# Sparse attention scores two heads at a time, low-key products in row halves, values eight units behind

## The chip, the cores and the metric

The kernel runs on one core of a Trainium2 chip. The core has five engines that work from instruction queues of their own: TensorE (PE in the profile; its weight loads are listed as PEld), VectorE (DVE), ScalarE (ACT), GpSimd (POOL) and SyncE (SP), which here issues nearly all DMA transfers. Each engine takes its instructions in a fixed order and waits at the first one whose inputs or buffers are not ready. The metric is the time of one execution on the device, in microseconds (us); lower is better.

## The reference

Two identical layers work on 512 tokens of width 1024. Each mixes three branches, adds them under sigmoid gates, and goes on to a gated feed-forward network of width 2816. The branches are two chunked gated linear attentions (HGRN2 with 4 heads of 128, GLA with 4 heads of 64) and a sparse attention of 8 heads of 64 in 2 key groups. The sparse attention is what the change is about. Cut to its core:

```python
for a block of 128 queries, t its token numbers:                     # 4 blocks
    p_c = masked_softmax(q @ kc, cmp_end <= t);  o_c = p_c @ vc      # 31 compressed keys
    # 16 blocks of 64 keys may be chosen, and 512 tokens have only 8: all of the past is chosen
    p_s = masked_softmax(q @ k_sel, tok <= t);   o_s = p_s @ v_sel   # "selected" branch
    p_w = masked_softmax(q @ k_win, causal);     o_w = p_w @ v_win   # "window" branch (512 wide)
out = gates[0]*o_c + gates[1]*o_s + gates[2]*o_w                     # per token and head
m = g[0]*(y_hg @ w_br_hg) + g[1]*(y_gla @ w_br_gla) + g[2]*(y_nsa @ w_br_nsa)   # g = sigmoid(h @ w_mgate)
```

With 512 tokens the selected and the window branch both reduce to plain causal attention, each with its own keys and values.

## The kernel before, in words

All large products are done as three matrix products of rounded parts: a weight block is split into a high part (`whi`, ScalarE, L276) and the rest (`wlo`, VectorE, L277), the activations likewise, and `mm3` (L264 to L272) issues high·high, high·low and low·high into one PSUM bank of 128x512. These "dense" triples carry the names of what they compute: `mmmgate` is a block of the branch gates' product, `mmbr2d` one of the product that takes the sparse attention's result into the branch sum. They are chained to one another in the order in which the program issues them; everything else is put among them by the framework's list scheduler when the program is built. It fixes one order for each engine, by priorities, its own cost estimates and the dependencies that the program adds by hand (`after`, L260). At run time nothing overtakes.

The sparse attention of a layer (`nsa`) first computes the compressed branch and its importance terms, then runs 48 score units. A unit is one head and one or both key branches for one block `i` of 128 queries: 8 units of 256 columns (block 0), 8 of 512 (block 1), 16 of 384 (block 2) and 16 of 512 (block 3). A unit's `scores` are the product of the stacked query with the keys. The query tile `xt` (`QS`) holds 128 rows for a head: rows 0 to 63 the rounded query (high), rows 64 to 127 what the rounding left (low). The key tiles (`lv`) hold the high keys `KH` in both row halves and the low keys `KL` in both, so one pass of 128 rows over `KH` gives (high + low query)·KH, and a second over `KL` adds (high + low query)·KL (L909). A small matmul then adds the causal mask to the last 128 columns (L911). The result lies in a bank with the tag `s`, of which there are two. VectorE takes the row maximum (L914), ScalarE the exponential and its sum (L130), and the weighted probabilities are written as a high and a low f16 part (`ahl`; ScalarE L923, VectorE L924). A DMA on SP's queue transposes `ahl` into `lr` (L931, in `turn`); `lr` has six buffers. `values` multiplies `lr` with the values, 12 small matmuls for each 512 columns (L939). `LAG2 = 5` puts the values of a unit behind the scores of the unit five later: each of their matmuls is made to follow that unit's last mask.

The values of a block are summed in one bank, taken by turns from the tags `o` and `t`. `stop` (L945) ends the sum with a matmul by zeros (L947), scales it on ScalarE (`og`, L949), transposes it with four matmuls into an `s` bank (L952) and splits it into the two `at` tiles (L954 ScalarE, L955 VectorE), which `mmbr2d` reads as soon as block 3 is done. Ahead of each zero matmul, `fill(PLAN["nsa"][i])` issues some of the queued steps (gate products of 24 matmuls, branch products of 12, or both) that the scheduler may lay beside the score units. The weight blocks of these steps arrive in two `wraw` buffers by DMAs (L173) that stand on SP's queue among the transpositions.

Of the kernel before, what the change touches and what calls it, by code (L numbers as in the profile page):

```python
# [9 lines left out]
F32 = mybir.dt.float32  # L10
# [10 lines left out]
P = 128  # L21
T = 512
# [40 lines left out]

LAG1, LAG2 = 0, 5
PLAN = {"hg": 4, "gla": (3, 1, 1, 1), "prep": (2,), "nsa": (2, 4, 6, 24)}
# [19 lines left out]
class Kernel:  # L85
    def __init__(self, ctx, tc, io):
        self.tc, self.nc, self.io = tc, tc.nc, io
        self.cp = ctx.enter_context(tc.tile_pool(name="cp", bufs=1))
        self.sb = ctx.enter_context(tc.tile_pool(name="sb", bufs=1))
        self.pp = ctx.enter_context(tc.tile_pool(name="pp", bufs=1, space=MS.PSUM))  # L90
        self.dp = ctx.enter_context(tc.tile_pool(name="dp", bufs=1, space=MS.DRAM))
        self.uid = 0
        self.base = 0
        self.ready = {}
        self.dense_last = None
# [5 lines left out]
    BUFS = dict(gss=2, gtot=2, ge=2, gsc=2, ginv=3, xt=1, og=2, xg=8, wraw=2, whi=2, wlo=2, y=16, nd=3, lq=8, ld=4, g=1, nm=2, sums=6, f=2, ahl=4, lr=6, w1=2, w2=2, w3=2,  # L101
                at=2, lv=2, v1=1, v2=1, v3=1, acc=1, rb=1, sc=1,
                mm=4, s=2, t=1, o=1)

# [217 lines left out]
    def rstd(self, acc, tokens):  # L322
        nc = self.nc
        with self.hp():
            ss = self.pt("t", [P, T])
            nc.tensor.matmul(ss, self.ones, acc, start=True, stop=True)
            rb = self.st("rb", [P, T])
            self.act(rb, ss, AF.Ln, scale=1.0 / D, bias=self.eps)
            self.act(rb, rb, AF.Exp, scale=-0.5)
            rs = None  # L330
            if tokens:
                ss = self.pt("t", [P, NT])
# [27 lines left out]
    def fit(self, xs, junk=None):  # L360
# [3 lines left out]
        for i, x in enumerate(xs):  # L364
            nc.scalar.activation(self.st("w3", list(x.shape), BF) if junk is None else junk, x, AF.Square, accum_out=acc[:, i:i + 1])
        ps = self.pt("t", [P, n])
        nc.tensor.matmul(ps, self.ones, acc, start=True, stop=True)
# [89 lines left out]
    def finish(self, o, g, inv, kc, x, tag):  # L457
# [4 lines left out]
        nc.scalar.activation(sq, o, AF.Square, scale=inv)  # L462
        ss = self.pt("t", [P, T])
        nc.tensor.matmul(ss, self.ones, sq, start=True, stop=True)
# [52 lines left out]
    def layer(self, l, x, sp):  # L517
# [88 lines left out]
        for r in range(2):  # L606
# [5 lines left out]
            nc.sync.dma_start(gw2, io["gw2"][l])  # L612
            ps = self.pt("t", [P, T])
            mm(ps, gw2[:, r * P:(r + 1) * P], glrT, start=True, stop=True)
# [13 lines left out]

        yn = self.nsa(l, sp, Bg, rs, QS, *v12, sg, fill)
        for d in range(KD):  # L630
# [90 lines left out]
    def small(self, l, xg, rs):  # L721
# [24 lines left out]
        nc.vector.tensor_scalar(ni, inv, 1.0 / S14, None, op0=ALU.mult)  # L746
        ps = self.pt("t", [16, T])
        for i in range(NT):
# [5 lines left out]
    def nsa_q(self, Bg, rs):  # L754
        nc, tp = self.nc, self.nc.tensor.transpose
        QS = self.st("xt", [P, 8, T], F32R)
        ps = Bg("n1")
        for i in range(NT):
            nd = self.spread(ps[i], rs, i)
            self.rope(nd, i, 8)  # L760
            c = slice(i * P, (i + 1) * P)
            for hh in range(2):
                pt = self.pt("t", [P, 4, P])
# [8 lines left out]
    def nsa(self, l, sp, Bg, rs, QS, v1, v2, sg, fill):  # L772
        nc, io = self.nc, self.io
# [7 lines left out]
        for i in range(NT):  # L781
            nd = self.spread(ps[i], rs, i)
            self.rope(nd, i, 6)
            pt = self.pt("t", [P, 4, P])
            for n in range(4):
# [4 lines left out]
            nc.vector.tensor_tensor(kl, kv, kh.bitcast(F32), op=ALU.subtract)  # L790
            pt = self.pt("t", [P, 4, P])
            for n, h in enumerate((0, 1, 6, 7)):
# [13 lines left out]
        for n in range(2):  # L806
            pt = self.pt("t", [64, P])
            for pc in range(16):
# [16 lines left out]
            nc.vector.tensor_tensor(z, z, xx, op=ALU.mult)  # L825
            pt = self.pt("t", [P, 2, 32])
            tp(pt.rearrange("p g n -> p (g n)"), z, self.ident[0:64, 0:64])
# [9 lines left out]
        for g in range(2):  # L837
            pt = self.pt("t", [P, 32])
            mm(pt, sp["w2k"], hidT[0][:, g, 0], start=True, stop=True)
# [15 lines left out]
            nc.scalar.activation(sct, ps, AF.Copy)  # L855
            pt = self.pt("t", [P, NT, 4, 32])
            for i in range(NT):
# [3 lines left out]
                self.cf["cmpb"].rearrange("p (i u n) -> p i u n", i=NT, u=1).to_broadcast([P, NT, 4, 32]), op=ALU.add)  # L861
            pt = self.pt("t", [P, 64])
            mm(pt, hidT[1][:, g].rearrange("p r n -> p (r n)"), sp["w2v"], start=True, stop=True)
# [21 lines left out]
        for i in range(NT):  # L885
            pt = self.pt("t", [P, 2, P])
            for g in range(2):
# [11 lines left out]

        def scores(u):  # L900
            i, h, brs = u["i"], u["h"], u["brs"]
            if u["new"]:
                start(i)
            g, n, nb = h // 4, len(brs), (i + 1) * P
            q = QS[:, h, i * P:(i + 1) * P]
            ps = self.pt("s", [P, i + 1, n, P])
            b0 = brs[0]
# [37 lines left out]
        def stop(i):  # L945
            fill(PLAN["nsa"][i])
            mm(Os[i], self.zero, v1[:, 0:2], start=False, stop=True)  # L947
            Y = self.st("og", [P, 8, 64])
# [5 lines left out]
            nc.scalar.activation(yh[:, :, c], pt, AF.Copy)  # L954
            nc.vector.tensor_tensor(yl[:, :, c], pt, yh[:, :, c].bitcast(F32), op=ALU.subtract)  # L955

        units = []
        for i in range(NT):
            us = [dict(i=i, h=h, brs=brs, new=False, last=False)
                  for h in range(8) for brs in (((0, 1),) if i < 2 else ((0,), (1,)))]  # L960
# [12 lines left out]
        return [(yh[:, c], yl[:, c]) for c in range(4)]  # L973

    def final(self, l, x, acts):
# [22 lines left out]
        for h in range(2):  # L998
# [7 lines left out]
            nc.scalar.activation(sq, x[:, last, c], AF.Square)  # L1006
            ss = self.pt("t", [P, W])
            nc.tensor.matmul(ss, self.ones, acc[:, c], start=True, stop=False)
# [121 lines left out]
```

## Time and profile before

| | us |
|---|---|
| median of 3 runs | 1976.72 (1970.16 to 1976.89) |
| the profiled execution: its time / its span | 1976.97 / 1975.2 |
| PE busy in the span | 1921.8 (97%) |
| DVE / ACT busy | 1189.5 (60%) / 1015.5 (51%) |
| first to last score of layer 0 / of layer 1 | 122.40 / 127.20 |
| the stretch behind it, to within the branch products that read its result, each layer | 27.60 |

The granted clock over the run is 0.995 of full. In the trace, "L939" is a line of the program, "t<-v,lr" says that the tile `t` is written from `v` and `lr`, "128*128 128x512" are the weights' and the moving operand's sizes, and "[1.03 <-ACT og L949]" says that the engine stood still for 1.03 us until ScalarE's instruction of line 949 was done.

### The profile page before, as it was taken

To read this page: it belongs to the slowest core of one execution; us is meant where nothing else is said; L and a number is where in the kernel's file an instruction comes from. 1 tells how busy PE (TensorE), PEld (TensorE's weight loads), DVE (VectorE), ACT (ScalarE), POOL (GpSimd) and SP (SyncE) were. 2 spreads that over 40 slices of the span, in tenths; PEclk is the share of its full clock that TensorE was granted. 3 is DMA by queue.
4 is the path that set the end of the run, shared out by engine and by line. 5 is a ranking of instruction groups with operands and counts; after the bars stand their busy time and mean duration, and the time that the engine had idled before them with its cause. 6 is when DMAs were issued, how large, how long until landed. Compare 5 with 4: busy or idle time off the path is not lost.

```text
span 1975.2 us, 27838 instructions
## 1 busy us (share of the span) xinstructions
PE 1921.8 (97%) x10706; PEld 1367.4 (69%) x10706; DVE 1189.5 (60%) x2409; ACT 1015.5 (51%) x1817; POOL 35.3 (2%) x82
## 2 busy tenths in 40 slices
PE   8999999999999999999999999999999999999998
PEld 6778776777678544468887877768766784444787
DVE  5768768668855644433347887676777565444233
ACT  5556544358844755422245556443778447553222
POOL 0000000000000000000000000000000000000000
PEclk9999999999999999999999999999999999999999
DMA  4222212326643633123332222222378335330232
GB/s 159 79 60 84 75 55 70 113 73 146 142 133 98 203 105 98 43 61 111 117 96 69 67 83 65 64 86 91 78 138 169 114 93 206 98 106 22 75 96 94
DMA packets 142293, 194.23 MB, mean 98 GB/s; under 512 B 91408, under 2 KB 94032, under 8 KB 142160
## 3 DMA queue, kind: packets, MB, share of 16 engines
q1 hardware_dynamic: 141584, 191.80, 33.9%
q8 instruction: 84, 1.38, 0.3%
q10 hardware_dynamic: 576, 0.66, 0.1%
q14 instruction: 49, 0.40, 0.1%
HBM read 167.25 MB, written 4.19 MB: 87 GB/s over the span
## 4 chain that ended last, share of the span: by engine, by line
PE 82%; DVE 10%; DMA 4%; ACT 2%; issue 2%; SPq 0%; DVEq 0%; ACTq 0%
PE mmf L268 8%; PE mmf L266 8%; PE mmf L267 8%; PE mm L268 6%; PE mm L267 6%; PE mm L266 6%; DMA lr<-ahl 4%; PE mmmgate L267 3%; PE mmmgate L266 3%; PE mmmgate L268 3%; DVE wlo L277 2%; PE o L453 2%; DVE ahl L410 2%; DVE at L432 1%; PE s L909 1%
## 5 line engine op out<-in xcount | busy, mean ns | idle before, releaser
L276 ACT ACTIVATE whi<-wraw 128x1024 fp32r<-128x1024 f32 (+3 forms) x242 | 232.4, 960 | 346.2 <-PE mm L267 112.8
L277 DVE TENSOR_TENSOR wlo<-wraw,whi 128x1024 fp32r<-128x1024 f32 (+3 forms) x242 | 266.4, 1101 | 176.4 <-ACT whi L276 175.2
L266 PE MATMUL mmmgate<-xg,whi 128*128 128x512 f32 x384 | 157.2, 409 | 0.0
L267 PE MATMUL mmmgate<-xg,whi 128*128 128x512 f32 x384 | 155.2, 404 | 0.0
L268 PE MATMUL mmmgate<-xg,wlo 128*128 128x512 f32 x384 | 153.5, 400 | 0.0
L212 DVE SCALAR_TENSOR_TENSOR whi<-xg,gsc,whi 128x1024 f16<-128x1024 f32 x38 | 48.8, 1284 | 139.5 <-ACT whi L211 139.5
L408 ACT ACTIVATE ahl<-lq 128x256 f16<-128x256 f32 x168 | 65.6, 425 | 85.0 <-DVE lq L412 54.8
L188 ACT ACTIVATE v<-xg 128x1024 bf16<-128x1024 f32 x76 | 79.9, 1051 | 33.1 <-DMA xg<-w 32.6
L267 PEld LDWEIGHTS mmmgate<-xg,whi 128*128 128x128 f32 x384 | 72.7, 189 | 15.8 <-issue 3.5
L266 PEld LDWEIGHTS mmmgate<-xg,whi 128*128 128x128 f32 x384 | 72.9, 190 | 14.4 <-ACT ld L130 0.7
L211 ACT ACTIVATE wlo<-xg,gsc 128x1024 f16<-128x1024 f32 x38 | 43.5, 1146 | 75.2 <-PE mmf L268 75.2
L268 PEld LDWEIGHTS mmmgate<-xg,wlo 128*128 128x128 f32 x384 | 72.6, 189 | 12.8
L130 ACT ACTIVATE ld<-s,nm 128x128 f32<-128x128 f32 (+3 forms) x128 | 65.7, 516 | 16.9 <-DVE nm L914 9.7
L914 DVE TENSOR_REDUCE nm<-s 128x1 f32<-128x384 f32 (+3 forms) x96 | 57.2, 596 | 27.0 <-PE s L911 26.1
L659 DVE SCALAR_TENSOR_TENSOR ld<-mmf,ginv,ld 128x512 f32<-128x512 f32 x40 | 30.0, 750 | 71.9 <-PE mmf L268 71.9
L268 PE MATMUL mmn<-whi,xg 128*128 128x512 f32 (+1 forms) x192 | 72.6, 378 | 0.0
L266 PE MATMUL mmn<-whi,xg 128*128 128x512 f32 (+1 forms) x192 | 70.8, 369 | 0.8 <-DVE og L483 0.8
L923 ACT ACTIVATE ahl<-ld,sums 128x128 f16<-128x128 f32 (+3 forms) x128 | 66.2, 552 | 9.9 <-DVE sums L920 2.9
L267 PE MATMUL mmn<-wlo,xg 128*128 128x512 f32 (+1 forms) x192 | 71.0, 370 | 0.0
L410 DVE TENSOR_TENSOR ahl<-lq,ahl 128x256 f16<-128x256 f32 x168 | 67.8, 426 | 2.9 <-ACT ahl L408 2.4
L924 DVE SCALAR_TENSOR_TENSOR ahl<-ld,sums,ahl 128x128 f16<-128x128 f32 (+3 forms) x128 | 66.4, 545 | 4.0 <-ACT ahl L923 3.4
L130 ACT ACTIVATE ld<-mmf,ginv 128x512 f32<-128x512 f32 x40 | 27.4, 684 | 70.3 <-PE mmf L268 70.2
(444 smaller groups left out, 5043.7 us busy)
## 6 DMA issues: line engine op xcount, KB each, us to landing
wraw<-w SPq DMA_DIRECT2D x188, 512.0 KB, 3.6
xg<-w SPq DMA_DIRECT2D x76, 512.0 KB, 3.6
wraw<-w SPq DMA_DIRECT2D x57, 256.0 KB, 2.6
xt<-xT SPq DMA_DIRECT2D x16, 256.0 KB, 5.3
lr<-cw SPq DMA_DIRECT2D x16, 256.0 KB, 3.7
xd<-xt SPq DMA_DIRECT2D x8, 256.0 KB, 2.6
xt<-xd SPq DMA_DIRECT2D x8, 256.0 KB, 3.8
out<-lq SPq DMA_DIRECT2D x8, 256.0 KB, 2.2
```

The costliest lines, as they stand in the source:

```text
L130: i = self.nc.scalar.activation(out, in_, func, **kw)
L188: self.nc.scalar.activation(self.st("v1", list(x.shape), BF), x, AF.Square, scale=scale, accum_out=ss)
L266: first = mm(out, a[0], b[0], start=start, stop=False)
L267: mm(out, a[0], b[1], start=False, stop=False)
L268: last = mm(out, a[1], b[0], start=False, stop=stop)
L276: nc.scalar.activation(hi, x, AF.Copy)
L277: nc.vector.tensor_tensor(lo, x, hi.bitcast(F32), op=ALU.subtract)
L408: nc.scalar.activation(y, x, AF.Copy)
L410: nc.vector.tensor_tensor(z, x, y, op=ALU.subtract)
L914: nc.vector.tensor_reduce(nm, pv, axis=AX.XY, op=ALU.max, negate=True)
L923: nc.scalar.activation(ahl[:, 0, b], a[:, b], AF.Copy, scale=sums[:, b:b + 1])
L924: nc.vector.scalar_tensor_tensor(ahl[:, 1, b], a[:, b], sums[:, b:b + 1], ahl[:, 0, b], op0=ALU.mult, op1=ALU.subtract)
```

## The change

Queries: for the odd heads the high and low query halves change places, so that an even head has its high query in rows 0 to 63 and an odd head in rows 64 to 127; one VectorE instruction of 64x512 (L768) becomes two of 64x256. Scores: two heads are taken in one run, with the order fixed by hand: the high-key pass of the second head, that of the first, then the low-key pass of the first and of the second, each with only the 64 rows of the high query (the two heads lie in different row halves; low query·KL is left out), then the masks of both. PSUM: the tag `t` is gone, its users take `s`, which has three banks instead of two; the value sums use `o` alone. Values: `LAG2` is 8, counted from the pair's last mask, and `lr` has nine buffers. End of the sparse attention: the last queued gate product is issued behind the last zero matmul, and a dependency added in `mm3` keeps its first matmul behind that one.

```diff
-LAG1, LAG2 = 0, 5
+LAG2 = 8
...
-    BUFS = dict(... lr=6 ...
-                mm=4, s=2, t=1, o=1)
+    BUFS = dict(... lr=9 ...
+                mm=4, s=3, o=1)
...
         last = mm(out, a[1], b[0], start=False, stop=stop)
+        if self.hold is not None:
+            self.after(first, self.hold)
+            self.hold = None
...
-            ss = self.pt("t", [P, T])
+            ss = self.pt("s", [P, T])
...
                 nc.scalar.activation(q, pt, AF.Copy, scale=0.125)
-                nc.vector.scalar_tensor_tensor(q[64:], pt[64:], 0.125, q[64:].bitcast(F32),
-                                               op0=ALU.mult, op1=ALU.subtract)
+                for h in range(2):
+                    r = slice(64 - h * 64, 128 - h * 64)
+                    a, b = q[r, h::2], pt[r, h::2]
+                    nc.vector.scalar_tensor_tensor(a, b, 0.125, a.bitcast(F32), op0=ALU.mult, op1=ALU.subtract)
...
-            po = Os[i] = self.pt("ot"[i % 2], [P, 8, 64])
+            po = Os[i] = self.pt("o", [P, 8, 64])
...
-            for t, kk in enumerate((KH, KL)):
-                mm(ps, q, kk[:, g, 0:i + 1, b0:b0 + n], start=t == 0, stop=False)
-            for b in range(n):
-                u["end"] = mm(ps[:, i, b], self.ident_b, self.causal, start=False, stop=b == n - 1).ins.name
+            kh, kl = (t[:, g, 0:i + 1, b0:b0 + n] for t in (KH, KL))
+            for u in (ua, ub):
+                u["ps"] = self.pt("s", [P, i + 1, n, P])
+                u["q"] = QS[:, u["h"], i * P:(i + 1) * P]
...
+            for u in (ub, ua):
+                step(u["ps"], u["q"], kh, start=True, stop=False)
+            for u in (ua, ub):
+                r = slice(u["h"] % 2 * 64, u["h"] % 2 * 64 + 64)
+                step(u["ps"], u["q"][r], kl[r], start=False, stop=False)
+            for u in (ua, ub):
+                for b in range(n):
+                    step(u["ps"][:, i, b], self.ident_b, self.causal, start=False, stop=b == n - 1)
+            ua["end"] = ub["end"] = last
...
-            fill(PLAN["nsa"][i])
-            mm(Os[i], self.zero, v1[:, 0:2], start=False, stop=True)
+            fill(PLAN["nsa"][i] if i < NT - 1 else len(steps) - 1)
+            ins = mm(Os[i], self.zero, v1[:, 0:2], start=False, stop=True)
...
+            if i == NT - 1:
+                self.hold = ins.ins.name
+                fill(1)
...
-        for u in range(n + LAG2):
-            if u < n:
-                scores(units[u])
-            if 0 <= u - LAG1 < n:
-                turn(units[u - LAG1])
-            if 0 <= u - LAG2 < n:
-                values(units[u - LAG2])
+        for k in range(0, n + LAG2, 2):
+            two = units[k:k + 2]
+            if two:
+                scores(*two)
+            for u in two:
+                softmax(u)
+                turn(u)
+            if k >= LAG2:
+                for u in units[k - LAG2:k - LAG2 + 2]:
+                    values(u)
```

What this makes of PE's order in block 3 of layer 0: before, a unit is its pass over `KH` (`lv_3388`), its pass over `KL` (`lv_3389`) and its mask, and the values of the unit five earlier follow.

```order
L909 MATMUL s_5415<-lv_3388,xt_627 128x512
L909 MATMUL s_5415<-lv_3389,xt_627 128x512
L911 LDWEIGHTS ident_b
L911 MATMUL s_5415<-causal,ident_b 128x128
L939 LDWEIGHTS lr_4943
L939 MATMUL t_4900<-v_230_1659,lr_4943 128x64
```

After, two heads' banks (`s_5555`, `s_5556`) are written in one run, and the scheduler has put dense matmuls between the two passes over `KH` (now `lv_3396`; `KL` is `lv_3397`).

```order
L918 MATMUL s_5556<-lv_3396,xt_627 128x512
L267 MATMUL mmmgate_970_5837<-xg_143,whi_5839 128x512
L268 MATMUL mmmgate_970_5837<-xg_143,wlo_5840 128x512
L918 MATMUL s_5555<-lv_3396,xt_627 128x512
L918 MATMUL s_5555<-lv_3397,xt_627 128x512
L918 MATMUL s_5556<-lv_3397,xt_627 128x512
L918 LDWEIGHTS ident_b
L918 MATMUL s_5555<-causal,ident_b 128x128
L918 LDWEIGHTS ident_b
L918 MATMUL s_5556<-causal,ident_b 128x128
L963 LDWEIGHTS lr_5003
L963 MATMUL o_4881<-v_230_1667,lr_5003 128x64
```

The values that follow now are those of the unit eight earlier, and both low-key passes stand side by side. The second place is PE's order at the end of layer 0's sparse attention: before, the zero matmul (L947), the four transpositions (L952) and the first branch product follow one another directly.

```order
L268 MATMUL mmmgate_995_6014<-xg_161,wlo_6017 128x512
L947 LDWEIGHTS zero
L947 MATMUL t_4900<-v_230_1659,zero 128x512
L952 MATMUL s_6054<-cf,og_6052 128x128 x4
L266 MATMUL mmbr2d_1002_6061<-at_3851,whi_6063 128x512
L267 MATMUL mmbr2d_1002_6061<-at_3852,whi_6063 128x512
```

After, the held gate product `mmmgate_997` stands behind the zero matmul (now L971): five of its 24 matmuls ahead of the transpositions (now L976), the first row below being the zero matmul.

```order
L971 MATMUL o_4881<-v_230_1667,zero 128x512
L266 MATMUL mmmgate_997_6032<-xg_121,whi_6034 128x512
L267 MATMUL mmmgate_997_6032<-xg_121,whi_6034 128x512
L268 MATMUL mmmgate_997_6032<-xg_121,wlo_6035 128x512
L266 MATMUL mmmgate_997_6032<-xg_125,whi_6034 128x512
L267 MATMUL mmmgate_997_6032<-xg_125,whi_6034 128x512
L976 MATMUL s_6025<-cf,og_6023 128x128 x4
L268 MATMUL mmmgate_997_6032<-xg_125,wlo_6035 128x512
```

Nineteen more of that product follow before the first `mmbr2d`. In each layer 281 dense matmuls stand between the first and the last score matmul before, and 225 after; between the last score and the first `mmbr2d` there are 68 before and 123 after.

## Rows read from the trace of the kernel before

**Rows 1.** The page: busy time by engine, and one group of instructions.

```profile
PE 1921.8 (97%) x10706; PEld 1367.4 (69%) x10706; DVE 1189.5 (60%) x2409; ACT 1015.5 (51%) x1817; POOL 35.3 (2%) x82
...
L277 DVE TENSOR_TENSOR wlo<-wraw,whi 128x1024 fp32r<-128x1024 f32 (+3 forms) x242 | 266.4, 1101 | 176.4 <-ACT whi L276 175.2
```

**Rows 2.** Waits of PE over the span: total us, times, longest us.

```profile
PE s L426 <- DVE ahl L410: 12.4, 18, 1.7
PE o L939 <- DMA lr<-ahl: 8.3, 8, 2.4
...
PE t L939 <- DMA lr<-ahl: 7.0, 11, 1.4
PE s L952 <- ACT og L949: 2.1, 2, 1.0
PE mmbr2d L266 <- ACT at L954: 1.9, 2, 1.0
...
PE s L909 <- ACT ld L130: 0.6, 2, 0.3
```

**Rows 3.** Windows, first to last score: length, PE PEld DVE ACT POOL busy, PEclk.

```profile
418.00:540.40 122.40, 117.82 (x905) 88.88 (x904) 101.48 (x257) 97.77 (x245) 0.00 (x0) 0.99 0.62 131
...
1392.70:1519.90 127.20, 118.04 (x904) 88.85 (x903) 100.62 (x255) 97.44 (x244) 0.00 (x0) 0.99 0.62 124
```

**Rows 4.** Windows: first and last of four stretches; PEclk follows the POOL column.

```profile
506.40:509.70 3.30, 3.30 (x25) 2.25 (x25) 2.43 (x6) 2.48 (x4) 0.00 (x0) 0.50 0.00 0
...
1544.10:1547.40 3.30, 3.30 (x8) 2.65 (x9) 0.00 (x0) 0.36 (x1) 0.00 (x0) 0.50 0.00 0
```

**Rows 5.** Timeline of SP's queue in block 3 of layer 0: start, us.

```profile
495.50 0.33 SPq L173 DMA_DIRECT2D wraw<-w  x1
496.07 8.89 SPq L931 DMA_TRANSPOSE lr<-ahl  x6
```

**Rows 6.** The chain of waits there: start, us, what.

```profile
500.29 4.64 DMA lr<-ahl
```

**Rows 7.** PE's timeline at the end of layer 0's sparse attention: start, us.

```profile
559.15 0.39 PE L268 MATMUL mmmgate<-xg,wlo 128*128 128x512 f32 x1
...
560.74 0.39 PE L947 MATMUL t<-v,zero 128*128 128x512 f16 x1
562.16 0.65 PE L952 MATMUL s<-cf,og 128*128 128x128 f32 x4 [1.03 <-ACT og L949]
563.76 0.49 PE L266 MATMUL mmbr2d<-at,whi 128*128 128x512 f32 x1 [0.95 <-ACT at L954]
564.49 0.79 PE L267 MATMUL mmbr2d<-at,whi 128*128 128x512 f32 x1 [0.23 <-DVE at L955]
```

**Rows 8.** Score units by form: the row maximum, one for each unit.

```profile
L914 DVE TENSOR_REDUCE nm<-s x96: 398/614/693, 418.8 to 1520.4; 128x1 f32<-128x384 f32 x32, 128x1 f32<-128x512 f32 x32, 128x2 f32<-128x256 f32 x16, 128x2 f32<-128x512 f32 x16
```

**Rows 9.** PE's timeline in the linear attentions: two passes with 128 rows.

```profile
59.72 0.40 PE L266 MATMUL mmn<-whi,xg 128*128 128x512 f32 x1
59.95 1.02 PE L398 MATMUL s<-ld,ones 128*128 128x512 f32 x2
...
61.05 0.39 PE L268 MATMUL mmn<-whi,xg 128*128 128x512 f32 x1
```

**Rows 10.** The same for two heads with 64 rows each.

```profile
305.00 0.39 PE L266 MATMUL mmgog<-xg,whi 128*128 128x512 f32 x1
305.32 1.13 PE L398 MATMUL s<-ld,ones 64*128 64x512 f32 x4
...
306.72 0.39 PE L268 MATMUL mmgog<-xg,wlo 128*128 128x512 f32 x1
```

**Rows 11.** PE's timeline where dense matmuls follow f16 ones.

```profile
530.63 0.48 PE L267 MATMUL mmmgate<-xg,whi 128*128 128x512 f32 x1
530.94 0.40 PE L268 MATMUL mmmgate<-xg,wlo 128*128 128x512 f32 x1
```

**Rows 12.** Groups by form, block 3 of layer 0: the softmax of 512 columns.

```profile
L130 ACT ACTIVATE ld<-s,nm 128x512 f32<-128x512 f32 x14 | 9.5, 679 | 2.5 <-DVE nm L914 2.0 <-DVE sums L920 0.5
L924 DVE SCALAR_TENSOR_TENSOR ahl<-ld,sums,ahl 128x512 f16<-128x512 f32 x13 | 9.5, 746 | 0.7 <-ACT ahl L923 0.6
```

More of the change, by code (lines that the diff above doesn't have):

```diff
@@ L94, in __init__ @@
         self.ready = {}
-        self.dense_last = None
+        self.dense_last = self.hold = None
         self.act_ins = []
@@ L99, in __init__ @@
         self.table("natural_log_exp_and_others")
-    BUFS = dict(gss=2, gtot=2, ge=2, gsc=2, ginv=3, xt=1, og=2, xg=8, wraw=2, whi=2, wlo=2, y=16, nd=3, lq=8, ld=4, g=1, nm=2, sums=6, f=2, ahl=4, lr=6, w1=2, w2=2, w3=2,
+    BUFS = dict(gss=2, gtot=2, ge=2, gsc=2, ginv=3, xt=1, og=2, xg=8, wraw=2, whi=2, wlo=2, y=16, nd=3, lq=8, ld=4, g=1, nm=2, sums=6, f=2, ahl=4, lr=9, w1=2, w2=2, w3=2,
                 at=2, lv=2, v1=1, v2=1, v3=1, acc=1, rb=1, sc=1,
-                mm=4, s=2, t=1, o=1)
+                mm=4, s=3, o=1)
     def name(self, tag):
@@ L331, in rstd @@
             if tokens:
-                ss = self.pt("t", [P, NT])
+                ss = self.pt("s", [P, NT])
                 for i in range(NT):
@@ L365, in fit @@
             nc.scalar.activation(self.st("w3", list(x.shape), BF) if junk is None else junk, x, AF.Square, accum_out=acc[:, i:i + 1])
-        ps = self.pt("t", [P, n])
+        ps = self.pt("s", [P, n])
         nc.tensor.matmul(ps, self.ones, acc, start=True, stop=True)
@@ L462, in finish @@
         nc.scalar.activation(sq, o, AF.Square, scale=inv)
-        ss = self.pt("t", [P, T])
+        ss = self.pt("s", [P, T])
         nc.tensor.matmul(ss, self.ones, sq, start=True, stop=True)
@@ L612, in layer @@
             nc.sync.dma_start(gw2, io["gw2"][l])
-            ps = self.pt("t", [P, T])
+            ps = self.pt("s", [P, T])
             mm(ps, gw2[:, r * P:(r + 1) * P], glrT, start=True, stop=True)
@@ L627, in layer @@
             yg += self.attend(Q, K, F, [(0, 64, 2 * r), (64, P, 2 * r + 1)], Vg, done)
-        yn = self.nsa(l, sp, Bg, rs, QS, *v12, sg, fill)
+        yn = self.nsa(l, sp, Bg, rs, QS, *v12, sg, fill, steps)
         for d in range(KD):
@@ L746, in small @@
         nc.vector.tensor_scalar(ni, inv, 1.0 / S14, None, op0=ALU.mult)
-        ps = self.pt("t", [16, T])
+        ps = self.pt("s", [16, T])
         for i in range(NT):
@@ L762, in nsa_q @@
             for hh in range(2):
-                pt = self.pt("t", [P, 4, P])
+                pt = self.pt("s", [P, 4, P])
                 for h in range(4):
@@ L767, in nsa_q, with nsa @@
                 nc.scalar.activation(q, pt, AF.Copy, scale=0.125)
-                nc.vector.scalar_tensor_tensor(q[64:], pt[64:], 0.125, q[64:].bitcast(F32),
-                                               op0=ALU.mult, op1=ALU.subtract)
+                for h in range(2):
+                    r = slice(64 - h * 64, 128 - h * 64)
+                    a, b = q[r, h::2], pt[r, h::2]
+                    nc.vector.scalar_tensor_tensor(a, b, 0.125, a.bitcast(F32), op0=ALU.mult, op1=ALU.subtract)
         return QS
-    def nsa(self, l, sp, Bg, rs, QS, v1, v2, sg, fill):
+    def nsa(self, l, sp, Bg, rs, QS, v1, v2, sg, fill, steps):
         nc, io = self.nc, self.io
@@ L783, in nsa @@
             self.rope(nd, i, 6)
-            pt = self.pt("t", [P, 4, P])
+            pt = self.pt("s", [P, 4, P])
             for n in range(4):
@@ L790, in nsa @@
             nc.vector.tensor_tensor(kl, kv, kh.bitcast(F32), op=ALU.subtract)
-            pt = self.pt("t", [P, 4, P])
+            pt = self.pt("s", [P, 4, P])
             for n, h in enumerate((0, 1, 6, 7)):
@@ L806, in nsa @@
         for n in range(2):
-            pt = self.pt("t", [64, P])
+            pt = self.pt("s", [64, P])
             for pc in range(16):
@@ L825, in nsa @@
             nc.vector.tensor_tensor(z, z, xx, op=ALU.mult)
-            pt = self.pt("t", [P, 2, 32])
+            pt = self.pt("s", [P, 2, 32])
             tp(pt.rearrange("p g n -> p (g n)"), z, self.ident[0:64, 0:64])
@@ L837, in nsa @@
         for g in range(2):
-            pt = self.pt("t", [P, 32])
+            pt = self.pt("s", [P, 32])
             mm(pt, sp["w2k"], hidT[0][:, g, 0], start=True, stop=True)
@@ L855, in nsa @@
             nc.scalar.activation(sct, ps, AF.Copy)
-            pt = self.pt("t", [P, NT, 4, 32])
+            pt = self.pt("s", [P, NT, 4, 32])
             for i in range(NT):
@@ L861, in nsa @@
                 self.cf["cmpb"].rearrange("p (i u n) -> p i u n", i=NT, u=1).to_broadcast([P, NT, 4, 32]), op=ALU.add)
-            pt = self.pt("t", [P, 64])
+            pt = self.pt("s", [P, 64])
             mm(pt, hidT[1][:, g].rearrange("p r n -> p (r n)"), sp["w2v"], start=True, stop=True)
@@ L885, in nsa @@
         for i in range(NT):
-            pt = self.pt("t", [P, 2, P])
+            pt = self.pt("s", [P, 2, P])
             for g in range(2):
@@ L898, in start, with scores, step, softmax @@
                    vbd[g].rearrange("p r d -> p (r d)"), start=False, stop=False)
-        def scores(u):
-            i, h, brs = u["i"], u["h"], u["brs"]
-            if u["new"]:
+        def scores(ua, ub):
+            i, brs = ua["i"], ua["brs"]
+            if ua["new"]:
                 start(i)
[L904 to L907, printed above, removed]
-            for t, kk in enumerate((KH, KL)):
-                mm(ps, q, kk[:, g, 0:i + 1, b0:b0 + n], start=t == 0, stop=False)
-            for b in range(n):
-                u["end"] = mm(ps[:, i, b], self.ident_b, self.causal, start=False, stop=b == n - 1).ins.name
+            g, n, b0 = ua["h"] // 4, len(brs), brs[0]
+            kh, kl = (t[:, g, 0:i + 1, b0:b0 + n] for t in (KH, KL))
+            for u in (ua, ub):
+                u["ps"] = self.pt("s", [P, i + 1, n, P])
+                u["q"] = QS[:, u["h"], i * P:(i + 1) * P]
+            last = None
+            def step(*a, **k):
+                nonlocal last
+                ins = mm(*a, **k)
+                if last is not None:
+                    self.after(ins, last)
+                last = ins.ins.name
+            for u in (ub, ua):
[7 more added lines that the diff above has]
+            ua["end"] = ub["end"] = last
+        def softmax(u):
+            i, h, brs, ps = u["i"], u["h"], u["brs"], u["ps"]
+            n, nb, b0 = len(brs), (i + 1) * P, brs[0]
             pv = ps.rearrange("p j b c -> p b j c")
@@ L955, in stop @@
             nc.vector.tensor_tensor(yl[:, :, c], pt, yh[:, :, c].bitcast(F32), op=ALU.subtract)
+            if i == NT - 1:
+                self.hold = ins.ins.name
+                fill(1)
         units = []
         for i in range(NT):
-            us = [dict(i=i, h=h, brs=brs, new=False, last=False)
-                  for h in range(8) for brs in (((0, 1),) if i < 2 else ((0,), (1,)))]
+            us = [dict(i=i, h=p + h, brs=brs, new=False, last=False) for p in range(0, 8, 2)
+                  for brs in (((0, 1),) if i < 2 else ((0,), (1,))) for h in range(2)]
             us[0]["new"] = us[-1]["last"] = True
@@ L1006, in final @@
             nc.scalar.activation(sq, x[:, last, c], AF.Square)
-            ss = self.pt("t", [P, W])
+            ss = self.pt("s", [P, W])
             nc.tensor.matmul(ss, self.ones, acc[:, c], start=True, stop=False)
```

## The prediction

> **What bounds the kernel now.** I read the page first: PE is busy for 1921.8 of 1975.2 us [rows 1], so VectorE and ScalarE can only matter where PE stands still or slows down. The waits of PE come next, since they say for whom it stands still. Two belong to this change: 15.3 us (8.3 and 7.0) in which a value matmul waits for its transposed weights, and 4.0 us (2.1 and 1.9) at the end of each sparse attention, where the transpositions wait for ScalarE's scaled sum and the first branch product for their result [rows 2]. The windows then show the stretch itself: first to last score takes 122.40 and 127.20 us, with VectorE busy for about 101 and ScalarE for about 97 [rows 3]. That is 81% of their mean for VectorE, far above its 60% over the span, so here its pace is near. The same view, cut finer, shows four stretches of 3.4 us at a granted clock of 0.50, which is the 1.2 GHz level [rows 4]: two among the scores, and one behind each layer end. Each follows a PE wait: the first begins within 2 us of the end of the landing that starts at 500.29 and takes 4.64 us [rows 6], the others likewise behind a wait. At half speed 3.4 us do the work of 1.7, so each costs 1.7 us.
>
> Why the values wait is on SP's queue: the transpositions stand in order with the weight loads, which need a free `wraw` buffer. A load goes out at 495.50 and six transpositions follow in 8.89 us, 1.48 each [rows 5]; the one of 500.29 lands at 504.93 [rows 6].
>
> All sums go against the profiled execution's 1976.97 us, which is 1.77 over its span and 0.25 above the median of the runs.
>
> **Values eight units behind.** A layer has 48 units (96 in all, [rows 8]), so one takes about 122.40/48 = 2.55 us [rows 3]. Five units are 12.7 us from a unit's last mask to its values; the longest wait is 2.4 us [rows 2], so about 15.1 would have been enough. Eight units are 20.4 us at this pace, and 17.7 if the stretch shrinks to the 106.4 us worked out below. Both are above 15.1. Of the 15.3 us I take 12.0 as gone and leave 3.3, because a load that holds the queue holds several transpositions at once, and because behind the last score no later unit sets a distance. Ends: 0 (the transpositions only come later too, as they wait on the same queue) and -15.3. The two half-clock stretches among the scores go with the waits ahead of them: -3.4. What then comes next is the softmax, below.
>
> **The held gate product.** Before, the zero matmul starts at 560.74; dense matmuls follow each other at (560.74-559.15)/7 = 0.227 us. The waits behind it are 1.03, 0.95 and 0.23 us; the first branch matmul needs 0.73 to the second instead of 0.227, of which 0.23 is that wait, so 0.27 more [rows 7]. With the half-clock stretch of 1.7 that makes 4.2 us a layer; layer 1's waits are the other halves of the same totals [rows 2]. After, five matmuls of the gate product (1.1 us) cover the scaling, which kept PE 1.03 waiting, and nineteen (4.3 us) cover the 1.60 us from the transpositions to the first branch matmul. That leaves 2.7 us for one gate exponential (0.68 for 512 columns, [rows 12]) that ScalarE now has between, so nothing is late next. The product itself is only moved. I take -8.0 for both layers, keeping 0.4 for the change between matmul kinds. If the cover failed at the first wait alone, 2.1 would come back.
>
> **Two heads in one run.** Three pieces. First, the two low-key passes of a pair take the time of one if they run side by side. A pass over the keys has as many columns as the row maximum reads, so the 96 units have 16x256+16x512+32x384+32x512 = 40960 [rows 8]; half of them, in passes of 512 at 0.227 us, is 40x0.227 = -9.1. Second, a pair enters and leaves the f32 passes once instead of twice: behind f16 work the first dense matmul takes 0.31 to the next [rows 11], 0.08 over 0.227, so 48 pairs save -4.0. Third, what a visit to row halves costs. The linear attentions show it both ways: two passes of 128 rows stretch the distance between dense matmuls to 61.05-59.72 = 1.33 us [rows 9], and two heads' two passes with 64 rows each to 306.72-305.00 = 1.72 [rows 10]. So four half passes do run as two, and the visit costs 0.39 more for entering and leaving; 48 x 0.39 = +18.7. Together +5.6. Ends: -13.1 (entering is free here, since only the masks behind and not weights of another size follow) and +14.7 (no pass saved, the visit paid). I take +5.6, as [rows 10] show the nearest kind of visit.
> The trace shows 0.39 us for a visit [rows 9, 10]. The Trainium skill, "TensorEngine Tiling (Array Packing)", section "Key Properties", says likewise that changing the tiling mode drains TensorE, while its "Theoretical Speedup" gives a dimension of 64 a speedup of two, which would bring the -13.1.
>
> **What the softmax does to it.** A run needs two of three banks, where a unit needed one of two. The cover is what stands between runs: a bank is free when its maximum (0.69 for 512 columns, [rows 8]) and its exponential (0.68, [rows 12]) are done, 1.4 us behind the masks for the first and 2.1 for the second; pairs are 5.1 us apart now, of which a run takes some 1.5. So there are about 1.5 us to spare, and one split of 1.10 us in front [rows 1] fits, two don't. Today PE waits only 0.6 us in all for it [rows 2]. But the stretch gets denser: 281-225 = 56 dense matmuls go behind the last score (12.7 us), which with half each of the waits (6.0), the clock (1.7) and the pairs (+2.8) leaves 124.8-12.7-6.0-1.7+2.8 = 106.4 of the two layers' mean [rows 3]. VectorE's work falls by only 56/24 x 1.10 = 2.6 (one split of 128x1024 serves 24 dense matmuls), from 101.1 to 98.5, so its share goes from 81 to 93%. Some of its work does move out in front, as the first scores now come later. For new waits I take +2.0 a layer, +4.0; ends 0 and +12.
>
> **Without price.** The sums' single bank makes each block's start wait for the copy of the block before; four to six dense matmuls stand there as they did before the transpositions: 0, at most 3 x 1.0 a layer. VectorE's two half instructions for the queries: 0.40 instead of half of 0.69 [rows 8], so 32 x 0.05 = 1.7 if nothing covered them, but VectorE is 60% busy [rows 1]. The other users of `t` share three banks with the scores of the linear attentions; PE waits 12.4 us there for VectorE [rows 2], on inputs and not on banks: -0.5, ends -4 and +4.
>
> **Sum.** -12.0 -3.4 -8.0 +5.6 +4.0 -0.5 = -14.3, so 1962.7, and 1962.5 by the median.
>
> **The rivals.**
> A, the forecast: 1962.5, its own range 1954 to 1969. Chance 0.50.
> B, row halves at full speed: nothing is paid for the visits, -13.1 instead of +5.6, so 1944. For it: the half passes start side by side [rows 10]. Against it: the 0.39 us of the same rows. Chance 0.15. The rule that gives a dimension of 64 a speedup of two, named above, would bring this; the trace so far agrees with the drain.
> C, VectorE's pace takes the gain: its share cannot rise above 0.88, little over halfway to 93%, so the stretch is 98.5/0.88 = 111.9 instead of 106.4, 5.5 a layer, 11.0 instead of 4.0: 1970. For it: 81% already, with 0.6 us of waits only because PE was late itself. Against it: what moves out in front. Chance 0.24.
> D, slower: the banks hold nearly every run. Two passes of a run are chained, so a bank that is late stops PE with the first pass done and the values queued behind the masks. If a split of 1.10 us [rows 1] is in the way in two of three pairs, that is 48x0.73 = 35 instead of 4: 1994. It decides from (14.3+4.0)/48 = 0.38 us a pair on. Against it: the spare 1.5 us. Chance 0.11.
>
> **How the numbers follow.** A measurement of this kernel can tell about 0.5% from no change, 9.9 us. Faster by more (below 1967): all of B, nine tenths of A, little of C: 0.66. Within: most of C, a tenth of A and a small part of D: 0.24. Slower (over 1986.6): D: 0.10. The range runs from 1947, just above B, to 1977, above C, and leaves out about 0.2.
>
> **What the changed kernel's profile would show.** Right: waits of value matmuls for the transposition at 3 us or less in all; no stretch at 0.50 among the scores or behind the layer ends; no wait of the transpositions or of the first branch matmul; a pair's low-key passes starting side by side, with about 0.4 us lost around them. C or D would show as waits of score matmuls on ScalarE's exponential of 8 us and more, B as a run of four passes in 3 x 0.227. The forecast is wrong if the transpositions still make the values wait for 8 us or more, or if the half-clock stretches stay without a wait ahead of them.

## The result and the profile after

| | us | ratio to before, 95% interval |
|---|---|---|
| before, runs beside it | 1975.43 (1970.16 to 1976.89) | |
| after | 1957.26 (1954.12 to 1958.75) | 0.9911 [0.9887, 0.9934] |
| predicted | 1962.5 (1947 to 1977) | |

The change makes the kernel 18.2 us faster, 0.9%; the forecast was 14.2. It lies in the range, and it is case A. A second measurement of the changed kernel, beside the experiments, gave 1956.1 us and 0.9896 [0.9881, 0.9910]. The profiled execution took 1958.75 us, with a span of 1956.9. All waits and stretches below are those of one profiled execution of each kernel.

The page of the profile after: PE is busy for 10.7 us less in a span that is 18.3 shorter, so the shorter waits are only part of the gain ([rows 1] of before).

```profile
PE 1911.1 (98%) x10706; PEld 1367.6 (70%) x10706; DVE 1192.4 (61%) x2425; ACT 1012.9 (52%) x1817; POOL 34.5 (2%) x82
```

PE's waits after, as in [rows 2]: total us, times, longest. L963 is the value matmul (L939 before), L900 the start of a block's sum, L918 the scores.

```profile
PE s L429 <- DVE ahl L413: 14.0, 22, 1.1
...
PE o L963 <- DMA lr<-ahl: 6.3, 7, 2.6
PE o L900 <- ACT og L973: 3.5, 4, 1.3
PE s L918 <- ACT ld L130: 1.3, 2, 0.7
```

The waits for the transposition went from 15.3 to 6.3. Those of the transpositions on PE and of the first branch matmul (4.0) are off the list. New is L900: the one sum bank makes a block's start wait for ScalarE's copy of the block before.

The windows from first to last score, as in [rows 3]: VectorE's share is 87 and 89%, where it was 83 and 79%.

```profile
423.30:522.70 99.40, 95.81 (x777) 71.32 (x777) 86.59 (x235) 84.27 (x222) 0.00 (x0) 1.00 0.76 144
1393.20:1490.40 97.20, 95.55 (x777) 71.32 (x776) 86.53 (x235) 84.57 (x222) 0.00 (x0) 1.00 0.75 147
```

The stretches of half clock, as in [rows 4]. There are three, each 3.4 us as before; only the middle one is in a sparse attention, and it stands behind the last score. The two among the scores and the two behind the layer ends are gone.

```profile
332.40:335.70 3.30, 3.30 (x7) 1.99 (x7) 0.00 (x0) 0.66 (x2) 0.00 (x0) 0.50 0.02 5
530.40:533.70 3.30, 3.30 (x30) 2.26 (x29) 0.97 (x2) 1.18 (x3) 0.00 (x0) 0.50 1.01 256
1233.50:1236.80 3.30, 3.30 (x19) 2.27 (x18) 3.30 (x9) 1.71 (x3) 0.00 (x0) 0.50 0.11 7
```

That one begins at the end of the longest wait that is left. PE's timeline there, 8 us behind layer 0's last score, and in the chain of waits the landing that it waits for:

```profile
527.32 0.39 PE L266 MATMUL mmmgate<-xg,whi 128*128 128x512 f32 x1
530.28 0.79 PE L963 MATMUL o<-v,lr 128*128 128x64 f16 x12 [2.57 <-DMA lr<-ahl]
```

```profile
524.37 5.86 DMA lr<-ahl
```

The transposition went out 1.7 us behind the last score and took 5.86 us to land, where the median of the 96 is 3.4. Of the 6.3 us of waits for the transposition, 6.0 stand behind the last score of a layer; before, only 2.6 of 15.3 did.

The end of layer 0's sparse attention, as in [rows 7]: the zero matmul, the held gate product in front of and behind the four transpositions, and the branch product without a gap (0.23 us from start to start).

```profile
554.32 0.39 PE L971 MATMUL o<-v,zero 128*128 128x512 f16 x1
554.36 0.58 PE L266 MATMUL mmmgate<-xg,whi 128*128 128x512 f32 x1
...
555.74 0.65 PE L976 MATMUL s<-cf,og 128*128 128x128 f32 x4
556.15 0.48 PE L268 MATMUL mmmgate<-xg,wlo 128*128 128x512 f32 x1
...
560.35 0.39 PE L268 MATMUL mmmgate<-xg,wlo 128*128 128x512 f32 x1
560.58 0.40 PE L266 MATMUL mmbr2d<-at,whi 128*128 128x512 f32 x1
560.81 0.39 PE L267 MATMUL mmbr2d<-at,whi 128*128 128x512 f32 x1
```

A run of two heads in block 3 of layer 0: the first head's high-key pass and both low-key passes (the three of 490.46), then the masks.

```profile
490.46 0.94 PE L918 MATMUL s<-lv,xt 128*128 128x512 f32 x3 [0.73 <-ACT ld L130]
491.33 0.28 PE L918 MATMUL s<-causal,ident_b 128*128 128x128 bf16 x2
```

The three take 0.87 us from start to start; at 0.227 a pass, side by side and without any price, it would be 0.45.

### The profile page after: what moved, and what is told of

Read it like the earlier page. It is cut to its first block, busy times and chain, and to the rows that moved or that the text cites. A ratio compares the mean times of both kernels' runs of the same rounds, so it can differ in the third digit from the quotient of the medians.

```text
span 1956.9 us, 27871 instructions
## 1 busy us (share of the span) xinstructions
PE 1911.1 (98%) x10706; PEld 1367.6 (70%) x10706; DVE 1192.4 (61%) x2425; ACT 1012.9 (52%) x1817; POOL 34.5 (2%) x82
## 4 chain that ended last, share of the span: by engine, by line
PE 81%; DVE 11%; ACT 3%; DMA 3%; issue 2%; SPq 0%; DVEq 0%; ACTq 0%
PE mmf L268 8%; PE mmf L266 8%; PE mmf L267 8%; PE mm L268 6%; PE mm L266 6%; PE mm L267 6%; PE mmmgate L266 4%; PE mmmgate L267 4%; PE mmmgate L268 4%; DVE wlo L280 2%; PE s L918 2%; PE o L456 2%; DVE ahl L413 2%; DMA lr<-ahl 2%; DVE at L435 1%
## 5 line engine op out<-in xcount | busy, mean ns | idle before, releaser
L266 PE MATMUL mmmgate<-xg,whi 128*128 128x512 f32 x384 | 153.7, 400 | 0.0
L267 PE MATMUL mmmgate<-xg,whi 128*128 128x512 f32 x384 | 152.8, 398 | 0.0
L947 ACT ACTIVATE ahl<-ld,sums 128x128 f16<-128x128 f32 (+3 forms) x128 | 66.5, 554 | 9.7 <-DMA lr<-ahl 3.9
```

The costliest lines, as they stand in the source:

```text
L947: nc.scalar.activation(ahl[:, 0, b], a[:, b], AF.Copy, scale=sums[:, b:b + 1])
```

## The experiments

Each kernel was timed in five rounds against the kernel before on the same chip, four kernels to a chip; the kernel before had medians of 1975.91, 1976.26 and 1976.16 us there.

**Low-key passes of 128 rows** in the changed kernel.

```diff
-                r = slice(u["h"] % 2 * 64, u["h"] % 2 * 64 + 64)
-                step(u["ps"], u["q"][r], kl[r], start=False, stop=False)
+                step(u["ps"], u["q"], kl, start=False, stop=False)
```

> The changed kernel with the low-key passes at the full 128 rows again (both query halves times the low keys, as before the change), the two-head run, its order and all else kept. Theory 1 (entering and leaving the row halves costs about what the shared pass saves): in the changed kernel the first pass in front of a visit takes 0.33 instead of 0.23 us and the pair of half passes 0.43 instead of 0.24, 0.29 us a pair, 13.9 in 48 pairs; the shared pass saves 9.1. So this kernel should be about 5 us faster than the changed one: 1952. Rival (the row halves are where the gain over the forecast came from): about 9 us slower than the changed one: 1966.

Measured: 1955.6 us, 0.9895 [0.9882, 0.9907]. That is 0.5 to 1.7 below the two measurements of the changed kernel, which can't be told apart by time. The rival's +9 is out; theory 1's -5 is not shown by the time (-0.5 to -1.7). The trace shows the run of two heads in block 3 with full rows:

```profile
490.02 0.97 PE L918 MATMUL s<-lv,xt 128*128 128x512 f32 x3 [0.92 <-ACT ld L130]
490.82 0.23 PE L918 MATMUL s<-causal,ident_b 128*128 128x128 bf16 x1
```

0.80 us instead of 0.87. Summed over all score matmuls, from each start to the next on PE and without waits and half clock, it is 49.7 us instead of 53.8: 4.1 less on PE, of which the time shows little. Its score matmuls wait 2.4 us for the softmax where they waited 1.3.

**Both heads in the same row half.**

```diff
-                r = slice(u["h"] % 2 * 64, u["h"] % 2 * 64 + 64)
+                r = slice(0, 64)
```

> The changed kernel with the low-key passes of both heads in row half 0 to 63, so that they stand one behind the other; the odd heads so multiply their low query with the low keys, a part of the result that differs. Theory 1 (the two half passes of the changed kernel run fully side by side and share one pass's time): 40 passes of 0.227 us come back, +9, 1965. Rival (the pair's time is set by filling and draining, and what the second pass takes is hidden in it): +0 to +4, 1956 to 1960.

Measured: 1962.02 us, 0.9936 [0.9922, 0.9949], +5 to +6. The run takes 1.10 us:

```profile
489.77 1.17 PE L918 MATMUL s<-lv,xt 128*128 128x512 f32 x3 [0.77 <-ACT ld L130]
490.87 0.28 PE L918 MATMUL s<-causal,ident_b 128*128 128x128 bf16 x2
```

That is 0.23, one pass, more than in the changed kernel, and the score sum is 62.6 instead of 53.8, +8.8. So the half passes of the changed kernel do overlap in full; of the 8.8 us the time shows some 3 less. In the profiled execution the waits at L900 were 1.9 us instead of 3.5, and there was one half-clock stretch instead of three, so part of the price came back elsewhere.

**No held product** in the changed kernel.

```diff
-            fill(PLAN["nsa"][i] if i < NT - 1 else len(steps) - 1)
+            fill(PLAN["nsa"][i])
...
-            if i == NT - 1:
-                self.hold = ins.ins.name
-                fill(1)
```

> The changed kernel without the held gate product: all steps are issued ahead of the last zero matmul, as before. Theory 1: the waits behind the last zero matmul come back (2.2 us a layer) with a half-clock stretch behind each (1.7 a layer) and 0.3 a layer of slower steps: +8, 1965. Rival (the 55 more dense matmuls behind the last score would have covered this anyway, or the stretch moves elsewhere): +0 to +3, 1957 to 1960.

Measured: 1964.5 us, 0.9940 [0.9928, 0.9952]: +7.2 to +8.4. The waits are back, with half-clock stretches at 527.8, 561.9 and 1507.4 us; the two of the changed kernel outside the sparse attention, at 332.4 and 1233.5, are not in this profile:

```profile
PE s L976 <- ACT og L973: 2.1, 2, 1.0
PE mmbr2d L266 <- ACT at L978: 1.9, 2, 1.0
```

**The held product alone**, in the kernel before, with the lines of the change's diff.

> The kernel before with the held gate product alone. Theory 1: the waits of the transpositions and of the first branch matmul go (4.5 us) and the two half-clock stretches behind them (3.4): -8, 1968. Rival (the held product is missing ahead of the zero matmul, where the last values then wait longer for their transposition): -2 to -4, with 2 us or more of new waits there.

Measured: 1967.05 us, 0.9957 [0.9945, 0.9969], -8.9. PE's waits there: the two for ScalarE are gone, and the values wait 15.0 us where it was 15.3. The two half-clock stretches behind the layer ends are gone too; two among the scores stay (538.4 and 1470.3), and a new one stands outside, at 1227.9.

```profile
PE o L942 <- DMA lr<-ahl: 8.4, 10, 2.7
...
PE t L942 <- DMA lr<-ahl: 6.6, 10, 1.8
```

**Values four units behind** in the changed kernel.

```diff
-LAG2 = 8
+LAG2 = 4
```

> The changed kernel with the values four units behind instead of eight (four is the nearest to the five of before that a run of two allows; nine buffers kept). Theory 1 (the distance decides): waits of value matmuls for the transposition of 15 us or more instead of 6.3, with two or more half-clock stretches: +12, 1969. Rival (the transpositions are late because of their queue, whatever the distance): waits stay within 3 us of 6.3, 1958 to 1960.

Measured: 1977.93 us, 1.0008 [0.9999, 1.0017]: the whole gain of the change is gone, +21, more than theory 1's +12. The waits:

```profile
PE o L963 <- DMA lr<-ahl: 23.0, 35, 1.9
```

They are short and many, 35 instead of 7, and the half-clock stretches that theory 1 expected did not come; there is one, at 1309.9, outside the scores. So waits are not all of it: over the whole profile PE waits 49.1 us instead of 36.9. The order built for four units also puts other work in front of a dense matmul 57 and 51 times in the two layers' scores instead of 33 each, and the dense matmuls there take 13.5 us instead of 5.4 beyond 0.227 each (waits and half clock left out).

**Eight units and the hold, nothing else**, in the kernel before: `LAG1, LAG2 = 0, 8`, `lr=9`, and the lines of the hold. One head at a time, two sum banks.

> The kernel before with the values eight units behind, nine transposed buffers and the held gate product, and nothing else: scores one head at a time, sums by turns in two banks, two score banks. Theory 1 (distance and hold carry the gain, the two-head run and the banks are about even): the hold gave -8.9 alone, the waits for the transposition fall from 15.3 to about 6 (-9) and two half-clock stretches among the scores go (-3.4): 1955 to 1957. Rival (the two-head run itself makes the dense matmuls cheaper, by fewer changes between f16 and f32 work, some 5 us a layer): 1962 to 1967.

Measured: 1955.2 us, 0.9889 [0.9875, 0.9904], beside 1956.1 and 0.9896 for the changed kernel on the same chip, whose expectation was

> The changed kernel once more, for comparison on the same chip. All theories: 1957, ratio 0.991.

Distance and hold alone give the whole gain. The rest of the change, two heads in one run, row halves and banks, is even: +0.9 us, inside either interval. The rival is out by the time, though its mechanism is there, as the next section shows. The values' waits are close to those of the changed kernel, and all stand behind a layer's last score:

```profile
PE t L942 <- DMA lr<-ahl: 5.8, 5, 1.9
```

**The new banks alone**, in the kernel before.

```diff
-                mm=4, s=2, t=1, o=1)
+                mm=4, s=3, o=1)
...
-            po = Os[i] = self.pt("ot"[i % 2], [P, 8, 64])
+            po = Os[i] = self.pt("o", [P, 8, 64])
```

(and `s` for every other `t`).

> The kernel before with the PSUM banks of the changed kernel and nothing else: no tag t, three banks s, every block's sum in the bank o. Theory 1 (the single sum bank makes the start of each block wait for the scaled copy of the one before, 3.5 us in the changed kernel; the third s bank gives little): +3 to +6, 1979 to 1982. Rival (three shared banks free the linear attentions, -0.5 in the prediction, and the start stays covered): 1972 to 1976.

Measured: 1978.77 us, 1.0017 [1.0006, 1.0027], +2.6: slower, by a little less than theory 1 said, and not for its reason. No start of a sum waits here; the values wait 20.5 us for their transposition instead of 15.3, and of the four half-clock stretches the two among the scores are gone:

```profile
PE o L939 <- DMA lr<-ahl: 20.5, 22, 2.2
```

**The sum started late** in the changed kernel.

```diff
-            if ua["new"]:
-                start(i)
...
+            ins = mm(po, self.zero, v1[:, 0:2], start=True, stop=False)
+            self.after(ins, <the last mask of the pair eight units on>)
...
             i, h, brs, aT, nb = (u[k] for k in ("i", "h", "brs", "aT", "nb"))
+            if u["new"]:
+                start(i)
```

> The changed kernel with the sum of a block started only where its first values stand, behind the masks eight units on. Theory 1 (the 3.5 us of waits for the scaled copy are lost time): no such waits, -3.5, 1953. Rival (PE is held there by the softmax in any case, and the waits turn up at the scores or values): within 1 us of the changed kernel, 1956.

Measured: 1953.96 us, 0.9894 [0.9880, 0.9908]. The waits at L900 are gone from the trace. The time is 2.1 to 3.3 us below the changed kernel's two measurements, but the intervals overlap, so by time alone this is not settled.

**Three versions that build on this.** The first has 128-row low-key passes, the late start, and in the last iterations gate products ahead of the values:

```diff
+            if k >= n:
+                fill(2 if k == n else 1)
...
+                        if u["at"] + LAG2 >= len(units):
+                            self.after(ins, self.dense_last.name)
```

> The changed kernel with low-key passes of 128 rows, and two more edits for the waits that the changed kernel shows: the sum of a block is started only where its first values stand (behind the masks eight units on), and one of the queued gate products is issued ahead of each of the last value groups, which are made to follow it. Theory 1 (the waits that are left are a matter of cover): the 3.9 us of waits for the scaled sum and 4 to 5 of the 5.9 for the transposition go, with one half-clock stretch (1.7) behind the longest: -9 against the kernel with 128 rows alone, 1947. Rival (the dense work is only moved, and the same waits come at the end of the stretch, behind the last zero matmul): 1954 to 1957.

Measured: 1951.97 us, 0.9878 [0.9862, 0.9895]: 3.6 us below the version with 128 rows alone, of theory 1's 9, with overlapping intervals. The waits at L900 went, those of the values rose to 7.7, 4.3 of them in layer 0. The chain there has the last softmax ending at 532.3, some 8 us behind the last score, with a gate exponential of ScalarE (`y`) among the steps before it, and then a landing.

```profile
529.08 0.61 ACT y L130
529.69 0.68 ACT ld L130 x2
530.88 0.68 ACT ahl L945
531.58 0.76 DVE ahl L946
532.35 0.24 SPq L953
532.68 6.32 DMA lr<-ahl
```

But this landing ends a wait of only 0.63 us. The longest wait of the layer comes earlier, for a transposition that went out at 525.25, and no half-clock stretch follows it:

```profile
530.26 0.52 PE L963 MATMUL o<-v,lr 128*128 128x64 f16 x12 [2.48 <-DMA lr<-ahl]
```

The second adds the same fill to the kernel with eight units and the hold:

> The kernel before with the values eight units behind, the held gate product and the gate products ahead of the last value groups. Theory 1: 4 to 5 us below the kernel with distance and hold alone, about 1951. Rival of there (the two-head run carries 10 us): 1958 to 1962.

Measured: 1953.82 us, 0.9882 [0.9867, 0.9897], with 7.0 us of waits for the transposition: the fill alone brings 1.4 of the 4 to 5, within the intervals nothing. The third sets the softmax of the last eight units ahead of the gates (`with self.hp():` around `softmax` and `turn`):

> The kernel best1 with the softmax of a layer's last eight units set ahead of the gates' exponentials. Theory 1 (the last transposition is late because ScalarE works off gates in front of the last softmax, which ends 10 us behind the last score): the waits of values fall from 7.7 to about 3 us: -4, 1948. Rival (SP's queue holds the last transpositions whenever their softmax ends): 7 us of waits stay, 1952.

Measured: 1949.59 us, 0.9872 [0.9858, 0.9885], the fastest of all, about 26.5 us below the kernel before and 6.5 to 7.7 below the changed one. The waits of its values:

```profile
PE o L963 <- DMA lr<-ahl: 4.8, 5, 1.8
```

The waits fell by 2.9 us, from 7.7, of theory 1's 4.7. The median is 2.4 below the first version's, on another chip, and the intervals overlap, so the time alone doesn't show this step.

## Why the prediction was right

The number came nearer than its terms: the gain from the distance was taken 3.5 us too high, and so was the cost of the two-head run with its banks, by 8.2. That one miss takes back a part of the other is luck.

**The held product** (-8.0): right in mechanism and size. Alone it gave -8.9, and without it the changed kernel loses 7.2 to 8.4. The waits (4.5) and the two stretches behind the layer ends come and go with it; stretches elsewhere came or went as well, which the term left out.

**Eight units** (-12.0 and -3.4 of clock): right in mechanism, 3.5 us too large. On top of the hold it gave 1955.2 - 1967.05 = -11.9 (each measured beside the kernel before, on two chips). Of the waits 9.2 went (15.0 to 5.8) instead of 12.0. Among the scores the distance did what was said: waits of 12.7 us before, 0.2 after. What was sized too low is the rest behind the last score, where no unit follows: 3.3 were left for it, and 5.1 to 6.0 stand there in the profiles of the changed kernel and of this one, where it was 2.6 before. The longest of them ends in the landing of 5.86 us shown above; why that one is so long is open. In the profile a half-clock stretch follows it, at 530.4, which the term didn't have.

**Two heads, softmax and banks** (+5.6, +4.0, -0.5, together +9.1): this is where the forecast missed most. Measured against the kernel with eight units and hold it is +0.9. By parts:
- The visit was taken at 0.39 us from [rows 9, 10]; here it costs less. With 128 rows the score sum is 4.1 lower, and the shared pass saves 8.8 (next point), so a visit costs (8.8+4.1)/48 = 0.27. In [rows 10] the visit ends in a dense matmul that has the next one 0.34 us behind it, 0.11 more than 0.227; here it ends in small masks. The working noted that difference only for the lower end.

```profile
306.38 0.50 PE L267 MATMUL mmgog<-xg,whi 128*128 128x512 f32 x1
306.72 0.39 PE L268 MATMUL mmgog<-xg,wlo 128*128 128x512 f32 x1
```

- The shared pass is real (+8.8 when it is taken away), as the first piece assumed with 9.1. Row halves are so a loss of 4.1 us on PE, not the gain of rival B. B's speedup of two held for the passes themselves, and entering and leaving took more than it back.
- Fewer changes between f16 and f32 work, costed at -4.0. Among the scores of a layer a dense matmul follows other work 46 times before, 47 times with eight units and the hold, and 33 times after; of these 33, 22 stand between the two high-key passes of a run, at 0.23 us, as in these rows of the changed kernel:

```profile
520.48 0.40 PE L267 MATMUL mmmgate<-xg,whi 128*128 128x512 f32 x1
520.72 0.39 PE L918 MATMUL s<-lv,xt 128*128 128x512 f32 x1
520.95 0.39 PE L268 MATMUL mmmgate<-xg,wlo 128*128 128x512 f32 x1
```

Beyond 0.227 each, waits and half clock left out, the dense matmuls among the scores of both layers take 12.0 us before, 12.1 with eight units and the hold, 12.9 with the new banks alone, and 5.4 after. So neither the distance nor the banks save anything here, and the two heads' run saves 6.7. Row halves (4.1), sum bank (3.5), waits at the scores (0.7) and two more half-clock stretches (3.4) take it back: +5.0 in all, where the spans of the two profiled executions differ by 5.2 and the medians on one chip by 0.9.

- The softmax's pace (+4.0) came as 1.3 us of waits at the scores, 0.7 more than before. VectorE's share did rise to 89%, below the 93% reckoned: it had 86.6 us of work in the stretch, not 98.5, in a stretch of 99.4 and 97.2 us, not 106.4. (The working's own figures add up to 107.2; nothing hangs on it.) Case C's ceiling of 0.88 did not hold back PE, nor did D's banks.
- The single sum bank was costed at 0 with at most 3 us a layer; it costs 3.5 in two layers as waits, four of the six starts behind another block. The cover named, four to six dense matmuls between L971 and L900, was there, and at those four it is 0.2 to 1.3 us too short.

**Outside the sparse attention** (-0.5): two half-clock stretches that the kernel before didn't have, at 332.4 and 1233.5, take 3.4. Each follows waits of 0.4 to 0.8 us for VectorE in the linear attentions; what brings them is open. The repeated run has them at 332.7 and 1302.1, the kernel with eight units and hold has none there, and one that keeps the bank `t` (the second of the three versions) has one at 256.5; so it isn't the banks alone. Nor is their number a fixed property of a kernel. Of the kernel before's executions beside the experiments, those with a mean granted clock of 0.998 took 1971.3 to 1973.7 us, and those with 0.994 took 1979.6 and 1981.4. At 1.7 us lost in a stretch, that is a difference of several stretches between executions of one kernel, so the clock terms of the forecast, read from one profile, are known to a few microseconds only.

**The signs that the prediction named.** The transpositions on PE and the first branch matmul wait no more, no half-clock stretch stands among the scores or behind the layer ends (the one at 530.4 lies between the two), and the low-key passes start side by side with 0.42 us around them, as said. The values' waits, 6.3 us, lie between the 3 that would have been right and the 8 that would have been wrong.

## What to carry to other kernels

A wait of an in-order engine is removed by distance or by cover, and both were priced from one trace to within 4 us: units of distance times the pace, and the held work's length beside the wait. Before a clever packing is added, price entering and leaving it at the place where it will stand, and test the rest of the change without it: here two small edits alone give the whole gain, and what the run of two heads saves in the dense matmuls is taken back elsewhere. Where the distance is counted in later units, look at the last ones, which have none behind them.

## What the runs showed of the hardware that was not expected

Two 64-row passes in different row halves run fully side by side (in one half they take 0.23 us more), and still a three-pass run is 0.07 us longer than with full rows (0.87 and 0.80). Many short waits came without half clock: with four units 35 waits of at most 1.9 us left no such stretch among the scores, where before 19 of at most 2.4 went with two. A stretch behind a wait costs 1.7 us on top, so in that profile the longest wait left (2.57) cost 4.3; in the first of the three versions a wait of 2.48 at the same place had no stretch behind it.
